# Weights split three groups ahead in five buffers, and the merge's bias tiles on SP's queue, in a hybrid RWKV and attention block

## Chip, cores and metric

The kernel runs on one core of a Trainium2 chip. The metric is the device time of one execution in microseconds (us); of several runs the median is given.

## What is computed

One residual layer on 256 tokens with 2048 channels, in float32. Two token mixers (RWKV-7 and banded chunk attention) share one normalised input and one large input projection; their gated outputs are projected, merged by sigmoid gates and projected once more.

```python
h = _rms_norm(x, pre_norm_g)
proj = h @ w_in                          # 2048 x 12288
p_r, p_k, p_v, z_r, q_a, k_a, v_a, z_a, m_r, m_a = split(proj)
y_r = _rwkv7_mixer(h, p_r, p_k, p_v, ...) * silu(z_r)
y_a = _chunk_band_attention(q_a, k_a, v_a, rel_bias) * silu(z_a)
u_r = y_r @ w_branch_rwkv;  u_a = y_a @ w_branch_attn
merged = sigmoid(m_r + b_merge[0]) * u_r + sigmoid(m_a + b_merge[1]) * u_a
x = x + _rms_norm(merged @ w_out, post_norm_g)
```

## The kernel before

All large products run on TensorE (PE) in float32r, and each float32 operand is split into a high part and a low part so that three products of the parts give the accuracy. The weights come from HBM in groups of 512 KB (four tiles of 128x256, or two of 128x512). One group goes through three hands: SP's queue loads it into a `raw` tile (`w_load`, line 87, `wide_chunks`, line 93; three buffers, NR), ScalarE (ACT) copies it to the high part `wh`, and VectorE (DVE) subtracts to get the low part `wl` (both in `split`, line 80). `wh` and `wl` have NH and NL buffers each. A `raw` tile comes free when both have read it, a pair `wh`, `wl` when PE has used it.

The products are listed in a plan (`product`, line 250) in this order: k0 and r0 (interleaved, on the un-normalised input), v0, lora (the low-rank decay and rate weights), then k, r and v of head pairs 2, 4 and 6, then the gates and the attention's q, k and v in the order of `ORDER`, then the merge (per 512 columns: mr, ma, ur, ua) and the output (o0 to o4). A name such as wh_k03 is the high part of group 3 of product k0; acc_k0 is its accumulator in PSUM. `run_plan` walks over the groups and, before the matmuls of group n, calls `prepare` for all groups up to n + 2. Between groups it pumps small steps of the recurrence and of the attention. The order on each engine in the built program is then set by a scheduler that works with a model of times of its own, so instructions of neighbouring groups can change places; on the chip each engine keeps the built order, and waits where an operand is late.

Names at the start: `hr_A`, `hr_yrl`, `hr_yrh` are the split raw input (16 tiles, from loads of `xT_UV` and `xT_R`), `hn` the normalised one, `lab`, `lab_Y`, `lab_s` the low-rank weights, `rb` and `rones` the norm's factor, `w2e`, `zw` and `lw` the decay's second product. In the middle, `SB` is the recurrent state, `pw` and `pu` products of its chain. In the merge, `bb` is a bias row of b_merge, spread over all partitions by the load (`load_bias`, line 949); it is added to the accumulator on line 967.

Of the kernel before, what the change touches and what calls it, by code (L numbers as in the profile page):

```python
# [9 lines left out]
F32 = mybir.dt.float32  # L10
# [12 lines left out]
BD = 1  # L23

NR = 3
NH = 4
NL = 4

ZI = 6

# [7 lines left out]
P = 128  # L38
D = 2048
# [22 lines left out]
def kernel(ctx: ExitStack, tc, x, xt, vecs, w_in, wa1, w2, a2, w0, rel, w_br, w_ba, w_out, post_g, bm, out):  # L62
    nc = tc.nc
# [5 lines left out]
    tp = ctx.enter_context(tc.tile_pool(name="tp", bufs=2))  # L69
# [4 lines left out]
    def small(name):  # L74
        return ps.tile([P, 512], F32, tag="sm", name=name)
# [4 lines left out]
    def split(h, l, src):  # L80
        ACT.activation(h, src, AF.Copy)  # L81
        DVE.tensor_tensor(l, src, h.bitcast(F32), op=ALU.subtract)  # L82
# [153 lines left out]
    def pump(n):  # L236
        nonlocal turn
        turn += 1
        step(side, n)
        if turn % BD == 0:  # L240
            step(back, BQ)
# [8 lines left out]
    def product(nm, raws, act, token_major, done=None, quota=1, before=None, wide=False, first=False):  # L250

        plan.append(dict(nm=nm, raws=raws, act=act, tm=token_major, done=done, quota=quota, before=before, wide=wide, first=first))
# [4 lines left out]
    def matmuls(acc, q, m, kk, k, wh, wl, first, last):  # L259
        a = q["act"](kk)  # L260
        ms = slice(m * P, (m + 1) * P)
        o = acc[:, m, 0:256]
        pair = not isinstance(a, tuple)
        if q["wide"]:
            wh, wl = (t.rearrange("p k c -> p (k c)").rearrange("p (k c) -> p k c", k=2) for t in (wh, wl))
            o = acc[:, m, :]
        if q["tm"]:
            ah, al = (a[:, 0, :], a[:, 1, :]) if pair else a
            ops = ((o, ah[:, ms], wh[:, k, :]), (o, ah[:, ms], wl[:, k, :]), (o, al[:, ms], wh[:, k, :]))
        elif pair:  # L270
            ops = ((acc[:, m, :], wh[:, k, ms], a.rearrange("p n t -> p (n t)")), (o, wl[:, k, ms], a[:, 0, :]))
        else:
            ops = ((o, wh[:, k, ms], a[0]), (o, wh[:, k, ms], a[1]), (o, wl[:, k, ms], a[0]))
        for n, (d, u, v) in enumerate(ops):
            PE.matmul(d, u, v, start=first and n == 0, stop=last and n == len(ops) - 1)  # L275

    def run_plan():

        steps = [(q, g) for g in range(4) for q in plan[:2]] + [(q, g) for q in plan[2:] for g in range(len(q["raws"]))]
        parts = {}  # L280

        def prepare(n):
            q, g = steps[n]
            if q is plan[-1] and g == len(q["raws"]) - 1:

                wh = bg.tile([P, 4, 256], F32R, tag="v", name="wh_last")
                wl = bg.tile([P, 4, 256], F32R, tag="bon", name="wl_last")
            else:
                wh, wl = (st.tile([P, 4, 256], F32R, tag=t, name=f"{t}_{q['nm']}{g}", bufs=n) for t, n in (("wh", NH), ("wl", NL)))
            raw = q["raws"][g]  # L290
            if hasattr(raw, "whole"):
                raw(wh, wl)
            else:
                split(wh, wl, raw())
            parts[n] = (wh, wl)

        ready = 0
        for n, (q, g) in enumerate(steps):
            while ready < len(steps) and ready <= n + 2:
                prepare(ready)  # L300
                ready += 1
            if g == 0:
                if q["before"]:
                    q["before"]()
                if q["first"]:
                    q["acc"] = small(f"acc_{q['nm']}").rearrange("p (m t) -> p m t", m=2)
                else:
                    q["acc"] = pm.tile([P, 2, 512], F32, tag="mm", name=f"acc_{q['nm']}")
            acc = q["acc"]
            ng = len(q["raws"])  # L310
            if q is plan[-1]:
                if g == ng - 1:
                    for m in range(2):

                        o = acc if not m else small("acc_last").unsqueeze(1).to_broadcast([P, 2, 512])
                        for kk in range(4 * ng):
                            matmuls(o, q, m, kk, kk % 4, *parts[n - ng + 1 + kk // 4], kk == 0, kk == 4 * ng - 1)
                        q["done"](o, m)
            elif q["wide"]:
                for m in range(2):  # L320
                    for k in range(2):
                        kk = 2 * g + k
                        matmuls(acc, q, m, kk, k, *parts[n], kk == 0, kk == 2 * ng - 1)
            else:
                if isinstance(q["act"](0), tuple) or q["tm"]:
                    cuts = [range(k, k + i) for k, i in FIRST] if n == 0 else (range(4),)
                else:

                    cuts = ()
                    wh, wl = parts[n]  # L330
                    for low in range(2):
                        for m in range(2):
                            for k in range(4):
                                a = q["act"](4 * g + k)
                                ms = slice(m * P, (m + 1) * P)
                                if low:
                                    PE.matmul(acc[:, m, 0:256], wl[:, k, ms], a[:, 0, :], start=False, stop=g == ng - 1 and k == 3)  # L337
                                else:
                                    PE.matmul(acc[:, m, :], wh[:, k, ms], a.rearrange("p n t -> p (n t)"), start=g == 0 and k == 0, stop=False)  # L339
                for ks in cuts:  # L340
                    for m in range(2):
                        for k in ks:
                            kk = 4 * g + k

                            one = q["first"]
                            matmuls(acc, q, m, kk, k, *parts[n], kk == 0 and (m == 0 or not one), kk == 4 * ng - 1 and (m == 1 or not one))
            if q is not plan[-1]:
                pump(q["quota"])
                if g == ng - 1 and q["done"]:
                    q["done"](acc)  # L350
# [580 lines left out]
    def start_merge():  # L931
        drain()
        mg.append(bg.tile([P, KT, T], F32R, tag="A", name="mgh"))
        mg.extend(bg.tile([P, KB, T], F32R, tag=t, name=f"mgl_{t}") for t in ("AB0", "yrl"))
# [11 lines left out]
    for c in range(4):  # L946
        ts = {}

        def load_bias(w, c=c, ts=ts):
            def f():  # L950
                if not (c or w):
                    start_merge()
                bb = tp.tile([P, 512], F32, tag="bb", name=f"bb{w}{c}")
                ts["b"] = bb
                nc.scalar.dma_start(bb, bm[w * D + c * 512:w * D + (c + 1) * 512].partition_broadcast(P))
                if not w:
                    if c % 2:
                        ts[0], ts[1] = (bg.tile([P, 2, 512], F32, tag=t, name=f"g{c}_{t}") for t in ("Y", "bon"))
                    else:
                        g = bg.tile([P, 2, 2, 512], F32, tag="yrh", name=f"g{c}")  # L960
                        ts[0], ts[1] = g[:, 0], g[:, 1]
            return f

        def dm(w, c=c, ts=ts):
            def f(acc):
                t = ts[w]
                DVE.tensor_tensor(t, acc, ts["b"].unsqueeze(1).to_broadcast([P, 2, 512]), op=ALU.add)
                ACT.activation(t, t, AF.Tanh, scale=0.5)
            return f

        def du(w, c=c, ts=ts):
            def f(acc):
                DVE.scalar_tensor_tensor(ts[w], ts[w], 1.0, acc, op0=ALU.add, op1=ALU.mult)
                if w:
                    DVE.tensor_tensor(ts[0], ts[0], ts[1], op=ALU.add)
                    back.append(turn_merged(c, ts[0]))
            return f

        def wide(nm, src, k0, act, done, before=None):
            product(nm, wide_chunks(src, k0, nm), act, True, done, before=before, wide=True)  # L980
        wide(f"mr{c}", w_in, O_MR + c * 512, h_norm, dm(0), load_bias(0))
        wide(f"ma{c}", w_in, O_MA + c * 512, h_norm, dm(1), load_bias(1))
        wide(f"ur{c}", w_br, c * 512, yr, du(0))
        wide(f"ua{c}", w_ba, c * 512, lambda k: ya[k // 4][:, k % 4], du(1))
# [93 lines left out]
```

## Time and profile before

| what | us |
|---|---|
| median of 3 runs (862.5, 862.61, 866.8) | 862.61 |
| the profiled execution's own time | 863.52 |
| its span, from first to last instruction | 861.8 |
| PE busy in the span | 842.4 |
| DVE busy | 572.6 |
| ACT busy | 425.4 |

The stages in the span: the start with k0, r0, v0, lora and k2 up to some 75 us, the other products of the mixers up to 490, the merge up to 764, the output product up to 854, and a tail of 8 us in which the last columns are normalised and stored. A busy share near one says that PE has work in flight, not that nothing could be faster. The views used below are the sums of each engine, PE's list of waits, stretches with the granted clock, and the instructions of one engine in order of time. A timeline row gives start, duration, engine, line, operation, operands with shapes, count, and in brackets the idle time ahead of it with what ended it.

### The profile page before, as it was taken

What the parts mean: (1) busy time and instruction counts of PE and PEld (TensorE: products, weight loads), DVE (VectorE), ACT (ScalarE), POOL (GpSimd) and SP (SyncE); (2) the same over time, 40 slices, a digit from 0 to 9 for tenths busy, and PEclk for the clock granted to TensorE, in tenths of its full rate; (3) what the DMA queues carried; (4) which work ended last, traced back from release to release, by engine and by line L of the source; (5) the groups of instructions that cost most, each with busy time, mean ns of one, the idle gap of its engine ahead of it and who ended that gap; (6) DMA issues with size and microseconds to landing.
All of it is one profiled execution on the core that took longest, in us unless ns stands there. A gap on an engine that the chain in (4) does not pass through costs nothing.

```text
span 861.8 us, 14000 instructions
## 1 busy us (share of the span) xinstructions
PE 842.4 (98%) x5624; PEld 714.7 (83%) x5624; DVE 572.6 (66%) x801; ACT 425.4 (49%) x600; POOL 17.2 (2%) x68
## 2 busy tenths in 40 slices
PE   7999999999899999999999999999999999999996
PEld 7998888888778888888888877888888888888896
DVE  7898996966647978645498776555564555565555
ACT  7558565536335554343456655444444444444442
POOL 2010000000000000000000000000000000000000
PEclk9999999999899999999999999999999999999999
DMA  9916634654243556633436545666666666675552
GB/s 296 249 46 194 195 124 137 198 170 133 72 125 99 172 154 208 201 123 123 146 124 197 170 130 172 205 181 204 208 195 198 202 206 225 221 251 197 194 187 99
DMA packets 119395, 149.35 MB, mean 173 GB/s; under 512 B 13601, under 2 KB 82209, under 8 KB 118946
## 3 DMA queue, kind: packets, MB, share of 16 engines
q1 hardware_dynamic: 114370, 139.48, 51.5%
q10 hardware_dynamic: 4960, 8.98, 3.3%
q8 instruction: 44, 0.72, 0.3%
q14 instruction: 21, 0.17, 0.1%
HBM read 145.82 MB, written 2.62 MB: 172 GB/s over the span
## 4 chain that ended last, share of the span: by engine, by line
PE 93%; DVE 2%; DMA 2%; SPq 1%; issue 0%; ACT 0%; DVEq 0%
PE acc_mr L275 10%; PE acc_ma L275 10%; PE acc_o L275 10%; PE acc_va L275 5%; PE acc_ua L275 5%; PE acc_ur L275 5%; PE acc_zr L339 4%; PE acc_q L339 4%; PE acc_za L339 3%; PE acc_ak L339 3%; PE acc_v L339 3%; PE acc_r L339 3%; PE acc_za L337 2%; PE acc_zr L337 2%; PE acc_q L337 2%; PE acc_k L339 2%
## 5 line engine op out<-in xcount | busy, mean ns | idle before, releaser
L275 PE MATMUL acc_mr<-wh_mr,hn 128*128 128x512 f32 x256 | 81.0, 392 | 0.0
L275 PE MATMUL acc_ma<-wh_ma,hn 128*128 128x512 f32 x256 | 79.9, 391 | 0.0
L82 DVE TENSOR_TENSOR wl_ma<-raw_ma,wh_ma 128x1024 fp32r<-128x1024 f32 x32 | 39.2, 1224 | 37.6 <-ACT wh_ma L81 37.6
L82 DVE TENSOR_TENSOR wl_o<-raw_o,wh_o 128x1024 fp32r<-128x1024 f32 x31 | 37.9, 1224 | 35.0 <-ACT wh_o L81 35.0
L82 DVE TENSOR_TENSOR wl_mr<-raw_mr,wh_mr 128x1024 fp32r<-128x1024 f32 x32 | 39.1, 1223 | 31.0 <-ACT wh_mr L81 30.9
L275 PEld LDWEIGHTS acc_mr<-wh_mr,hn 128*128 128x128 f32 x256 | 48.0, 188 | 10.3 <-issue 0.5
L275 PEld LDWEIGHTS acc_ma<-wh_ma,hn 128*128 128x128 f32 x256 | 47.8, 188 | 10.1 <-issue 0.3
L81 ACT ACTIVATE wh_ma<-raw_ma 128x1024 fp32r<-128x1024 f32 x32 | 33.9, 1060 | 42.8 <-PE acc_mr L275 17.5
L81 ACT ACTIVATE wh_mr<-raw_mr 128x1024 fp32r<-128x1024 f32 x32 | 33.9, 1061 | 42.1 <-PE acc_ua L275 18.1
L81 ACT ACTIVATE wh_o<-raw_o 128x1024 fp32r<-128x1024 f32 x31 | 32.9, 1060 | 41.6 <-PE acc_o L275 26.5
L275 PE MATMUL acc_mr<-wl_mr,hn 128*128 128x512 f32 x128 | 50.2, 392 | 0.0
L275 PE MATMUL acc_o<-wh_o,mgh 128*128 128x512 f32 (+1 forms) x140 | 49.9, 356 | 0.0
L275 PE MATMUL acc_ma<-wl_ma,hn 128*128 128x512 f32 x128 | 49.8, 389 | 0.0
L275 PE MATMUL acc_o<-wl_o,mgh 128*128 128x512 f32 (+1 forms) x140 | 49.8, 356 | 0.0
L275 PE MATMUL acc_va<-wh_va,hn 128*128 128x512 f32 x128 | 41.0, 398 | 0.0
L339 PE MATMUL acc_q<-hn,wh_q 128*128 128x512 f32 x128 | 34.0, 401 | 0.0
L339 PE MATMUL acc_zr<-hn,wh_zr 128*128 128x512 f32 x128 | 33.7, 402 | 0.3 <-DVE ak L384 0.3
L339 PE MATMUL acc_ak<-hn,wh_ak 128*128 128x512 f32 x128 | 33.6, 398 | 0.3 <-DVE aq L384 0.3
L339 PE MATMUL acc_za<-hn,wh_za 128*128 128x512 f32 x128 | 33.8, 398 | 0.0
L82 DVE TENSOR_TENSOR wl_ua<-raw_ua,wh_ua 128x1024 fp32r<-128x1024 f32 x16 | 19.6, 1223 | 18.0 <-ACT wh_ua L81 18.0
L82 DVE TENSOR_TENSOR wl_ur<-raw_ur,wh_ur 128x1024 fp32r<-128x1024 f32 x16 | 19.6, 1223 | 17.9 <-ACT wh_ur L81 17.9
L82 DVE TENSOR_TENSOR wl_va<-raw_va,wh_va 128x1024 fp32r<-128x1024 f32 x16 | 19.5, 1222 | 17.2 <-ACT wh_va L81 15.8
(481 smaller groups left out, 2094.5 us busy)
## 6 DMA issues: line engine op xcount, KB each, us to landing
raw_mr<-w_in_d SPq DMA_DIRECT2D x32, 512.0 KB, 4.5
raw_ma<-w_in_d SPq DMA_DIRECT2D x32, 512.0 KB, 3.6
raw_o<-w_out_d SPq DMA_DIRECT2D x32, 512.0 KB, 4.7
raw_v<-w_in_d SPq DMA_DIRECT2D x16, 512.0 KB, 3.7
raw_q<-w_in_d SPq DMA_DIRECT2D x16, 512.0 KB, 3.6
raw_ak<-w_in_d SPq DMA_DIRECT2D x16, 512.0 KB, 3.6
raw_zr<-w_in_d SPq DMA_DIRECT2D x16, 512.0 KB, 3.7
raw_va<-w_in_d SPq DMA_DIRECT2D x16, 512.0 KB, 3.6
```

Source lines behind the costliest of these rows:

```text
L81: ACT.activation(h, src, AF.Copy)
L82: DVE.tensor_tensor(l, src, h.bitcast(F32), op=ALU.subtract)
L275: PE.matmul(d, u, v, start=first and n == 0, stop=last and n == len(ops) - 1)
L337: PE.matmul(acc[:, m, 0:256], wl[:, k, ms], a[:, 0, :], start=False, stop=g == ng - 1 and k == 3)
L339: PE.matmul(acc[:, m, :], wh[:, k, ms], a.rearrange("p n t -> p (n t)"), start=g == 0 and k == 0, stop=False)
```

## The change

Three things change. `wh` and `wl` get five buffers each instead of four, and `prepare` runs up to group n + 3 instead of n + 2. The eight bias tiles of the merge leave their own tag `bb` (two buffers of 2 KB per partition) and take the two buffers of tag `xs`, which the token shift and the gates zr2, zr0 and zr4 used before. And their loads are issued on SP's queue, where the weights are loaded, instead of ACT's.

```diff
-NH = 4
-NL = 4
+NH = 5
+NL = 5
@@ run_plan
-            while ready < len(steps) and ready <= n + 2:
+            while ready < len(steps) and ready <= n + 3:
@@ load_bias
-                bb = tp.tile([P, 512], F32, tag="bb", name=f"bb{w}{c}")
+                bb = tp.tile([P, 512], F32, tag="xs", name=f"bb{w}{c}", bufs=2)
                 ts["b"] = bb
-                nc.scalar.dma_start(bb, bm[w * D + c * 512:w * D + (c + 1) * 512].partition_broadcast(P))
+                nc.sync.dma_start(bb, bm[w * D + c * 512:w * D + (c + 1) * 512].partition_broadcast(P))
```

Before, the loads of the first two bias tiles stand on ACT's queue among its first activations, ahead of wh_k00 and of wh_r00. After, they stand on SP's queue, the first ahead of the load raw_ak43, the second ahead of raw_za62, and the other six in the merge, some six groups ahead of the bias's use. On SP's queue at the start, the load raw_v02 now stands ahead of w2e and not behind it.

PE at the start, where k0 and r0 end and v0 begins, before:

```order
L275 MATMUL acc_r0_235<-hr_yrl_79,wl_r02_299 128x256
L275 MATMUL acc_k0_202<-hr_yrh_80,wh_k03_333 128x256 x2
L275 MATMUL acc_r0_235<-hr_yrh_80,wh_r03_371 128x256 x2
L275 MATMUL acc_k0_202<-hr_yrh_80,wl_k03_334 128x256
L275 MATMUL acc_k0_202<-hr_yrh_80,wh_k03_333 128x256 x2
```

The same place after:

```order
L275 MATMUL acc_r0_249<-hr_yrl_79,wl_r02_275 128x256
L275 MATMUL acc_k0_210<-hr_yrh_80,wh_k03_309 128x256 x2
L275 MATMUL acc_r0_249<-hr_yrh_80,wh_r03_347 128x256 x2
L275 MATMUL acc_v0_509<-hr_A_78,wh_v00_383 128x256 x2
L275 MATMUL acc_k0_210<-hr_yrh_80,wl_k03_310 128x256
L275 MATMUL acc_k0_210<-hr_yrh_80,wh_k03_309 128x256 x2
```

The first two matmuls of v0, which need wh_v00, moved from behind all 24 matmuls of group k03 to a place ahead of its low part. (In the same way the first two of r01 moved ahead of wl_k01, and `rb` moved some 14 matmuls back.)

DVE from the split of lora2 on, where the normalised input is made, before:

```order
L82 TENSOR_TENSOR wl_lora2_626<-lab_Y_379,wh_lora2_625 128x1024
L370 SCALAR_TENSOR_TENSOR xT_R_82<-xT_R_82,vt_75,rones_106 128x256 x2
L82 TENSOR_TENSOR hn_656<-xT_UV_81,hn_656 128x4x256
L370 SCALAR_TENSOR_TENSOR xT_R_82<-xT_R_82,vt_75,rones_106 128x256
L82 TENSOR_TENSOR hn_656<-xT_UV_81,hn_656 128x4x256
L82 TENSOR_TENSOR wl_lora3_664<-lab_s_380,wh_lora3_663 128x1024
L82 TENSOR_TENSOR hn_656<-xT_R_82,hn_656 128x4x256
```

After:

```order
L370 SCALAR_TENSOR_TENSOR xT_R_82<-xT_R_82,vt_75,rones_106 128x256
L82 TENSOR_TENSOR wl_lora3_632<-lab_s_356,wh_lora3_631 128x1024
L740 SCALAR_TENSOR_TENSOR r0_498<-xsr0_495,vt_75,r0_498 128x256 x2
L82 TENSOR_TENSOR hn_662<-xT_UV_81,hn_662 128x4x256
L370 SCALAR_TENSOR_TENSOR xT_R_82<-xT_R_82,vt_75,rones_106 128x256
L82 TENSOR_TENSOR wl_k20_670<-raw_k20_671,wh_k20_669 128x1024
```

The low part of lora3 moved ahead of all four splits of `hn`; it stood behind two of them. The splits of k20 to k23 moved up too, between those of `hn`.

PE where k2 ends, r2 begins and the decay's product `lw` stands, before:

```order
L275 MATMUL acc_k2_785<-hr_yrh_80,wh_k23_818 128x256 x2
L455 MATMUL lw00_810<-w2e_157,zw_158 128x512
L455 MATMUL lw01_814<-w2e_157,zw_158 128x512
L466 MATMUL pn0_862<-pn0h_858,onesr_112 128x512
L275 MATMUL acc_k2_785<-hr_yrh_80,wl_k23_819 128x256
L339 MATMUL acc_r2_968<-hn_656,wh_r20_878 128x512 x8
```

After:

```order
L275 MATMUL acc_k2_791<-hr_yrh_80,wh_k23_785 128x256 x2
L275 MATMUL acc_k2_791<-hr_yrh_80,wl_k23_786 128x256
L339 MATMUL acc_r2_974<-hn_662,wh_r20_824 128x512 x7
L455 MATMUL lw00_816<-w2e_157,zw_158 128x512
L455 MATMUL lw01_820<-w2e_157,zw_158 128x512
L466 MATMUL pn0_868<-pn0h_864,onesr_112 128x512
L339 MATMUL acc_r2_974<-hn_662,wh_r20_824 128x512
```

Seven matmuls of r20 moved ahead of `lw`. What makes `zw`, which `lw` reads, now has one more split ahead of it on each engine: wl_r21 on DVE, and wh_r22 on ACT. From k43 on, PE's order is the same as before up to the last product.

## Rows read from the trace of the kernel before

**Rows 1.** The profile's first part: busy time, share and instructions of each engine.

```profile
PE 842.4 (98%) x5624; PEld 714.7 (83%) x5624; DVE 572.6 (66%) x801; ACT 425.4 (49%) x600; POOL 17.2 (2%) x68
```

**Rows 2.** PE's waits by releaser: us in total, times, longest us.

```profile
PE pw L662 <- DVE SB L695: 1.8, 1, 1.8
PE acc_k L275 <- DVE wl_k L82: 1.6, 3, 0.8
PE acc_k L275 <- ACT wh_k L81: 1.5, 2, 1.2
...
PE lw L455 <- issue: 1.1, 1, 1.1
PE acc_lora L275 <- DVE wl_lora L82: 1.0, 1, 1.0
```

**Rows 3.** Stretches: busy PE, PEld, DVE, ACT, POOL; granted clock, DMA share, GB/s.

```profile
13.00:27.00 14.00, 13.24 (x108) 12.84 (x107) 12.25 (x19) 9.57 (x15) 0.00 (x0) 1.00 1.11 340
27.00:31.00 4.00, 2.68 (x18) 2.06 (x17) 3.49 (x5) 2.19 (x3) 0.00 (x0) 1.00 1.11 237
...
216.30:219.70 3.40, 1.44 (x31) 1.04 (x27) 3.32 (x7) 0.38 (x1) 0.00 (x0) 1.00 0.13 21
219.70:226.50 6.80, 6.16 (x83) 5.60 (x83) 6.15 (x13) 2.86 (x6) 0.00 (x0) 0.51 0.19 69
...
566.00:764.00 198.00, 198.00 (x887) 164.24 (x886) 108.42 (x93) 85.70 (x84) 0.00 (x0) 1.00 0.65 208
...
853.50:861.80 8.30, 0.43 (x4) 0.22 (x2) 3.77 (x7) 1.49 (x4) 1.46 (x1) 0.78 0.56 203
```

**Rows 4.** ACT in order of time, in the first 75 us.

```profile
4.46 0.35 ACTq L955 DMA_DIRECT2D bb<-bm_d  x1
...
6.12 0.41 ACTq L955 DMA_DIRECT2D bb<-bm_d  x1
...
24.64 1.71 ACT L145 ACTIVATE hr_yrh<-xT_R,vt 128x256 fp32r<-128x256 f32 x4 [3.15 <-DMA xT_R<-xt_d]
...
31.73 1.06 ACT L81 ACTIVATE wh_v<-raw_v 128x1024 fp32r<-128x1024 f32 x1 [2.54 <-DMA raw_v<-w_in_d]
...
72.62 0.42 ACT L424 ACTIVATE zw<-lz 64x256 f32<-64x256 f32 x1
```

**Rows 5.** Section 6 of the page: a DMA issue, its count, KB and us to landing.

```profile
bb<-bm_d ACTq DMA_DIRECT2D x8, 256.0 KB, 4.5
```

**Rows 6.** PE in order of time, at the start.

```profile
29.25 0.50 PE L275 MATMUL acc_r<-hr_yrh,wh_r 128*128 128x256 f32 x2 [0.44 <-ACT wh_r L81]
30.35 0.39 PE L275 MATMUL acc_k<-hr_yrh,wl_k 128*128 128x256 f32 x1 [0.60 <-DVE wl_k L82]
...
33.09 0.40 PE L275 MATMUL acc_v<-hr_A,wh_v 128*128 128x256 f32 x2
...
57.75 0.39 PE L275 MATMUL acc_lora<-hr_yrh,wl_lora 128*128 128x256 f32 x1 [1.04 <-DVE wl_lora L82]
...
73.13 1.96 PE L455 MATMUL lw<-w2e,zw 65*128 65x512 f32 x4 [1.10 <-issue]
...
75.28 1.99 PE L339 MATMUL acc_r<-hn,wh_r 128*128 128x512 f32 x8
```

**Rows 7.** DVE in order of time, at the start, near 217 us, and in the merge.

```profile
28.74 0.42 DVE L411 TENSOR_TENSOR lab_Y<-lab_Y,vt 128x256 f32<-128x256 f32 x1 [0.18 <-DMA lab_Y<-wa_d]
29.08 1.22 DVE L82 TENSOR_TENSOR wl_k<-raw,wh_k 128x1024 fp32r<-128x1024 f32 x1
...
56.49 1.21 DVE L82 TENSOR_TENSOR wl_lora<-lab_s,wh_lora 128x1024 fp32r<-128x1024 f32 x1
...
216.98 1.22 DVE L82 TENSOR_TENSOR wl_zr<-raw_zr,wh_zr 128x1024 fp32r<-128x1024 f32 x1
...
588.90 1.22 DVE L967 TENSOR_TENSOR g_Y<-acc_mr,bb 128x1024 f32<-128x1024 f32 x1 [0.40 <-PE acc_mr L275]
```

**Rows 8.** The chain that ended last, in the merge: start, duration, what.

```profile
588.86 21.76 PE acc_ma L275 x96
```

## The prediction, made before the changed kernel was run

> **What bounds the kernel.** I read the sums of the engines first. PE is busy for 842.4 of 861.8 us [rows 1], so all idle time of PE together is 19.4 us, and nothing in this change takes a matmul away. Then where these 19.4 us lie. After 853.5 us PE is busy for 0.43 of 8.30 [rows 3]: some 7.9 us are the tail after the last matmul, which the change does not touch. The rest, 11.5 us, is PE's list of waits; its largest entries [rows 2] lie at the start (weights of k0 and r0, lora's last group, `lw`) and at one place in the middle, where the recurrence waits for its state SB. The merge has no idle time at all: PE is busy for 198.00 of 198.00 us from 566 to 764 [rows 3]. A weight that is ready a group sooner is worth something only where PE waits for weights, and that is the start.
>
> One more loss stands in the stretches. From 219.7 to 226.5 us the granted clock is 0.51, which is the level of 1.2 GHz, and it is 1.00 (2.4 GHz) in every other stretch of rows 3 but the tail. Ahead of the fall PE had been busy for only 1.44 of 3.40 us, waiting for SB [rows 2, 3]. At half speed, 6.80 us give about 0.49 x 6.80 = 3.3 us less work. So the middle costs some 5 us, the wait and the clock together.
>
> **The sum's base.** The profiled execution took 863.52 us for a span of 861.8. The terms below are differences in the span, and I put them on the median of the runs, 862.61.
>
> **Steady state: nothing.** With five buffers and a lead of three groups, the split of group n+1 stands where that of group n stood, and waits for the same matmuls to free its buffers. DVE and ACT do the same work at the same times, on a group one later. That holds in the middle too. Before SB's update DVE still has a split to do, at the place of the one at 216.98 [rows 7]; it is now va00's and not zr23's, of the same size. So I leave the wait for SB and the fall of the clock as they are. What hides the third group of lead is that two were enough, outside of the start.
>
> **Term 1, the weights of k0, r0 and v0.** Two things act against each other. (a) The bias loads at 4.46 and 6.12 [rows 4] leave the start: 2 x 256 KB [rows 5], at the 340 GB/s that the DMA engines move from 13 to 27 us, with their share full [rows 3], are 1.5 us. What lands after some 13 us should land up to that much sooner, for instance the last input tiles, for which ACT waited 3.15 us until 24.64 [rows 4]. (b) PE's order is worse: the first two matmuls of v0 stand ahead of the low part of k03. Before, that low part began at 30.35, when DVE had made it, and v0 came at 33.09 [rows 6]. Now PE cannot pass v0 until wh_v00 is there; that activation began at 31.73 on the landing of raw_v00, and took 1.06 [rows 4], so 32.8 before. I bound it. Latest: no gain from (a), 32.8. Earliest: lab_Y lands at 28.7 [rows 7], raw_v00 follows 512 KB or 1.5 us later at the full rate (the rate fell to 237 GB/s there [rows 3], with w2e's load in the stream, which now comes one load later), less 1.5 from (a), plus 0.1 and 1.06 for ACT: 29.9. I take 30.4, nearer to the early end, because the stream was full until 27 us and the bias bytes were in it. Before, from 30.35 PE needed 33.09 - 30.35 = 2.74 us for the low stretch of k03 and 0.24 for v0's pair, done at 33.33. After, the pair comes first: 30.4 + 0.24 + 2.74 = 33.4. So term 1 is 0.0 us, with ends of -0.5 and +2.4. The gain from the bias loads is eaten by the order.
>
> By the Trainium skill (DMA: Bandwidth & Descriptors, "Issuing engines are not separate DMA queues"), loads issued by different engines run on the same 16 DMA engines and interleave. By that rule the change of queue would bring nothing by itself, and (a) would come wholly from the later time of the two loads; the full share in rows 3 agrees, and the sum stays.
>
> **Term 2, lora.** At 57.75 PE had waited 1.04 us for the low part of lora3 [rows 6]; DVE made it at 56.49, behind two splits of `hn` of 1.21 us each [rows 7]. It now stands ahead of both, 2.4 us sooner, which more than covers the wait: -1.04. What is late next are the splits of k20 to k23, which moved up as well.
>
> **Term 3, lw.** At 73.13 PE had waited 1.10 us [rows 6] for `zw`, made on ACT at 72.62 in 0.42 [rows 4]. Now seven matmuls of r20, of 1.99 / 8 = 0.25 us or a little less each [rows 6], some 1.6 us, stand ahead of it on PE as cover. Against it, `zw` has the split wl_r21 (1.2 us) and wh_r22 (1.06) more ahead of it. But these are fed by loads that can start only when k22 and k23 are split, and these splits come sooner. I take the cover as sufficient: -1.1. If both splits come at their old pace, `zw` is 2.3 us later, at 75.3; PE, with the 1.04 of term 2 and the 1.6 us of r20 done, stands in front of it, and of terms 2 and 3 together +0.6 is left (75.3 against 73.13 + 1.6 = 74.7). So the two together are -2.1, ends -2.1 and +0.6.
>
> **Term 4, the merge's loads.** Six loads of 256 KB, 0.75 us each at 340 GB/s, go through SP's queue among the weights, where PE has a lead of three groups of 21.76 / 8 = 2.72 us [rows 8]. I take 0, covered by that lead; without it, see the third rival.
>
> **Sum.** 0.0 - 1.0 - 1.1 = -2.1, so 862.6 - 2.1 = 860.5 us; by the bounds 862.6 - 2.6 = 860.0 to 862.6 + 3.0 = 865.6.
>
> **Rivals.** (1) The clock falls at the start; the slower side. Ahead of v0's pair PE would do only two pairs of matmuls (0.5 us) between about 27.9 and 30.4, so it is idle for some 2.0 of 2.5 us, and for longer if raw_v00 is late. Before, 1.32 of 4.00 us idle (27 to 31) left the clock at 1.00, and 1.96 of 3.40 idle (216.3 to 219.7) came ahead of its fall [rows 3]. [...] Price 3.3 us: 863.8, and with v0 at its latest, 866.2, slower than before. For it: the size of the idle stretch. Against it: the stretch is short if raw_v00 lands at the early end. (2) The fall in the middle is missed: PE comes to the wait for SB a few us sooner, and the clock stays up. -3.3: 857.2. [...] The Trainium skill (TensorE: Matmul & The Clock Gate, "What's actually happening") says that the gate's watch runs freely and does not start with the kernel; by that, the same idle stretch can bring a fall in one run and not in another, which no row here shows. (3) The bias loads hold up the weights. SP takes its queue in order, and a bias load waits for the DVE addition that frees its buffer (1.22 us, after the last matmul of a product [rows 7]); the next group's load is behind it. Where the lead of 8.2 us is used up, each of the six costs 1.2 + 0.75 = 2 us: 860.5 + 12 = 872.5. Against it: the next load has to wait for a split that ends about as late as that addition. By the Trainium skill (DMA: Bandwidth & Descriptors, "Anatomy of one DMA") a wait sits on the issuing sequencer and not in the DMA engines, which is the mechanism of this rival. (4) The lead does nothing: what PE gains until 75 us it waits for further on, since DVE paces the start. No change, 862.6.
>
> **How the numbers follow.** Forecast 0.42, rival 1 0.32, rival 2 0.14, rival 3 0.04, rival 4 0.08. The likeliest is 860.5. A range from 856.9 to 864.8 takes in rivals 1, 2 and 4 at their centres and leaves out rival 3 and the late end of rival 1. A measurement of this kernel can tell about 0.5%, or 4.3 us, from no change: faster is below 858.3, slower above 866.9. Faster has rival 2 and a rest of the forecast's low end, 0.18; slower has rival 3 and the late end of rival 1, 0.07; the same, 0.75.
>
> **What would show it.** Right: PE waits in front of v0's first pair near 28 to 30.4 us, with wh_v as the releaser; no wait at lora3; a wait under 0.5 us at `lw`; the same wait for SB and the same stretch at half clock near 215 to 225; 198 of 198 us busy in the merge. Wrong: a stretch at 0.5 of the clock after 30 us (rival 1), none near 220 (rival 2), PE idle in the merge behind a weight (rival 3), or waits for `wl` between 75 and 125 us (rival 4).

## The result and the profile after

The changed kernel took 859.0 us in the median of five runs (858.32 to 860.16), the kernel before 863.35 beside it: a ratio of 0.9946, with a 95% interval of 0.9928 to 0.9964. In a later group of runs (e5 below) it was 859.92 against 864.44, 0.9954 (0.9936 to 0.9972). So the kernel is about 0.5% faster, 4.4 us. The prediction had 860.5, a gain of 2.1 us on a base of 862.61 from three runs; the five runs beside the changed kernel put that base at 863.35. The time lies in the predicted range, the gain is twice as large. The profiled execution took 858.43 us for a span of 856.7, against 863.52 and 861.8 before.

The sums of the engines on the page of the changed kernel (busy time, share, instructions):

```profile
PE 839.7 (98%) x5624; PEld 712.5 (83%) x5624; DVE 571.3 (67%) x801; ACT 424.7 (50%) x600; POOL 18.2 (2%) x68
```

Busy PE fell by 2.7 us against [rows 1] with the same instructions, the idle time by 2.4 us (19.4 to 17.0). The stretches of the changed kernel, with the columns of [rows 3], and one more stretch at the start:

```profile
9.00:12.00 3.00, 2.23 (x17) 1.82 (x16) 2.16 (x3) 3.00 (x6) 0.00 (x0) 1.00 1.09 349
13.00:27.00 14.00, 13.93 (x114) 13.52 (x113) 13.61 (x22) 11.71 (x17) 0.00 (x0) 1.00 1.11 337
27.00:31.00 4.00, 2.83 (x24) 2.63 (x24) 4.00 (x5) 1.83 (x2) 0.00 (x0) 1.00 0.90 202
...
216.30:219.70 3.40, 2.12 (x52) 1.86 (x52) 3.09 (x7) 1.46 (x4) 0.00 (x0) 1.00 0.32 122
219.70:226.50 6.80, 6.61 (x71) 5.46 (x69) 4.17 (x8) 2.65 (x5) 0.00 (x0) 1.00 0.01 2
566.00:764.00 198.00, 198.00 (x888) 164.18 (x887) 105.86 (x92) 84.85 (x84) 0.00 (x0) 1.00 0.65 211
```

Three things differ from [rows 3]. DVE is busy for 13.61 of 14.00 us from 13 to 27 (12.25 before) and for all 4.00 from 27 to 31 (3.49 before): its data come sooner. PE is busy for 13.93 (13.24 before). And in this execution the granted clock is 1.00 from 216 to 226 us, where it was 0.51 from 219.7 on before. The merge is full in both.

PE's longest waits in the changed kernel (us in total, times, longest):

```profile
PE pw L662 <- DVE SB L695: 1.8, 1, 1.8
PE acc_k L275 <- ACT wh_k L81: 1.2, 1, 1.2
PE acc_v L275 <- ACT wh_v L81: 1.2, 1, 1.2
```

Against [rows 2], `lora` and `lw` have left the list, and the wait for wh_v in front of v0's first pair is new. Further down the list the wait for UV behind SB has grown from 0.2 to 1.0 us. ACT and then PE at the start, in order of time:

```profile
20.95 1.71 ACT L145 ACTIVATE hr_yrh<-xT_R,vt 128x256 fp32r<-128x256 f32 x4 [1.02 <-DMA xT_R<-xt_d]
...
27.86 1.06 ACT L81 ACTIVATE wh_v<-raw_v 128x1024 fp32r<-128x1024 f32 x1 [1.34 <-DVE wl_k L82]
...
70.61 0.42 ACT L424 ACTIVATE zw<-lz 64x256 f32<-64x256 f32 x1
```

```profile
28.97 0.51 PE L275 MATMUL acc_v<-hr_A,wh_v 128*128 128x256 f32 x2 [1.17 <-ACT wh_v L81]
29.32 0.28 PE L275 MATMUL acc_k<-hr_yrh,wl_k 128*128 128x256 f32 x1
...
31.95 0.28 PE L275 MATMUL acc_r<-hr_yrh,wl_r 128*128 128x256 f32 x1
...
55.17 0.28 PE L275 MATMUL acc_lora<-hr_yrh,wl_lora 128*128 128x256 f32 x1
...
69.33 1.77 PE L339 MATMUL acc_r<-hn,wh_r 128*128 128x512 f32 x7
71.13 1.96 PE L455 MATMUL lw<-w2e,zw 65*128 65x512 f32 x4
```

Read with [rows 4] and [rows 6]: the last input tiles are there 3.7 us sooner (20.95 against 24.64), wh_v begins at 27.86 and not at 31.73, PE reaches the low part of k03 1.0 us sooner (29.32 against 30.35) in spite of its 1.17 us in front of v0, passes lora3 2.6 us sooner and without a wait (55.17 against 57.75), and does seven matmuls of r20 ahead of `lw`, which then needs no wait. The fair place to compare the start is the low part of r03, since by then v0's pair and k03 are done in both orders. It begins at 31.95 after and at 33.33 before, 1.38 us sooner:

```profile
33.33 0.28 PE L275 MATMUL acc_r<-hr_yrh,wl_r 128*128 128x256 f32 x1
```

### The profile page after: what moved, and what is told of

Read it like the earlier page. It is cut to its first block, busy times and chain, and to the rows that moved or that the text cites. A ratio compares the mean times of both kernels' runs of the same rounds, so it can differ in the third digit from the quotient of the medians.

```text
span 856.7 us, 14014 instructions
## 1 busy us (share of the span) xinstructions
PE 839.7 (98%) x5624; PEld 712.5 (83%) x5624; DVE 571.3 (67%) x801; ACT 424.7 (50%) x600; POOL 18.2 (2%) x68
## 4 chain that ended last, share of the span: by engine, by line
PE 94%; DVE 2%; SPq 2%; DMA 1%; ACT 1%; issue 0%; DVEq 0%
PE acc_mr L275 10%; PE acc_ma L275 10%; PE acc_o L275 10%; PE acc_va L275 5%; PE acc_ua L275 5%; PE acc_ur L275 5%; PE acc_q L339 4%; PE acc_zr L339 4%; PE acc_za L339 3%; PE acc_ak L339 3%; PE acc_v L339 3%; PE acc_r L339 3%; PE acc_za L337 2%; PE acc_zr L337 2%; PE acc_q L337 2%; PE acc_ak L337 2%
## 5 line engine op out<-in xcount | busy, mean ns | idle before, releaser
L81 ACT ACTIVATE wh_ak<-raw_ak 128x1024 fp32r<-128x1024 f32 x16 | 16.9, 1058 | 29.1 <-PE acc_q L339 13.4
```

## The experiments

In each group of runs the kernel before ran on the same chip; its medians were 863.70 (e1 to e4), 864.44 (e5 to e8), 864.69 (e9 to e11) and 863.38 (e12). Ratios are to it. The changed kernel itself ran again only beside e6 to e8 (as e5), so e1 to e4 and e9 to e12 are set against it by way of these ratios. The edits are shown abridged.

| run | what | us | ratio, 95% interval |
|---|---|---|---|
| e1 | before, bias tiles moved only | 862.27 | 0.9981 (0.9967 to 0.9994) |
| e2 | changed, two early loads put back | 864.46 | 1.0011 (0.9994 to 1.0027) |
| e3 | changed, lead of two groups | 860.97 | 0.9961 (0.9946 to 0.9976) |
| e4 | changed, v0 behind k03 | 861.41 | 0.9981 (0.9967 to 0.9994) |
| e5 | changed, once more | 859.92 | 0.9954 (0.9936 to 0.9972) |
| e6 | changed, one split on POOL | 861.40 | 0.9971 (0.9961 to 0.9982) |
| e7 | before, one split on POOL | 864.49 | 1.0010 (0.9992 to 1.0028) |
| e8 | changed, bias on ACT's queue | 859.95 | 0.9950 (0.9930 to 0.9970) |
| e9 | changed, split behind UV | 857.99 | 0.9928 (0.9902 to 0.9953) |
| e10 | before, split behind UV | 863.44 | 0.9984 (0.9963 to 1.0006) |
| e11 | changed, lw ahead of r20 | 861.20 | 0.9970 (0.9949 to 0.9991) |
| e12 | e9 and r * k behind UV | 859.90 | 0.9950 (0.9932 to 0.9969) |

### e1 and e2: the bias loads alone, and the fifth buffers alone

e1 is the change without its first half (NH and NL are 4, the lead is two). e2 is the changed kernel with the two early loads back:

```diff
+    early = bg.tile([P, 2, 512], F32, tag="AB0", name="early")
@@ first_raw
+                if g == 0:
+                    nc.scalar.dma_start(early[:, k // 2, :], bm[k * 256:k * 256 + 512].partition_broadcast(P))
                 split(wh[:, k:k + n, :], wl[:, k:k + n, :], raw[:, k:k + n, :])
```

> Four buffers and the old lead, as in the kernel before; only the bias tiles are moved (tag xs, SP's queue, out of the start). Theory (three separate gains at the start): only the loads' part is there. PE reaches the low part of k03 about 1.0 us sooner than before and stays 1.4 us sooner through v0; the wait for wl_lora3 (1.0 us) and for lw (1.1 us) are still there. Some 1.4 us less than before, 861.9 where before has 863.35. Rival (one gain: the early loads hold up everything that follows, and the rest is a consequence): lora and lw come 2.6 to 3.5 us sooner as in the changed kernel, 859.9.

> The changed kernel with two more loads of 256 KB each, issued on ACT's queue among its first activations, where the kernel before issued its first two bias loads, into a tile that nothing reads. Theory (three separate gains): the gain of the sooner landings goes, wl_k03 is back at about 30.4 us, while wl_lora3 still stands ahead of the splits of hn and has no wait (-1.0); lw stands without the matmuls of r20 ahead of it here, so its wait of some 1.1 us is back. 1 us less than before, 862.3. Rival (the order with five buffers carries the whole gain): as the changed kernel within 1 us, 859 to 860.

The time of e1 came out as the theory had it, 1.4 us less than before. The first row on ACT, and then PE at lora3 and in front of `lw`:

```profile
20.42 1.71 ACT L145 ACTIVATE hr_yrh<-xT_R,vt 128x256 fp32r<-128x256 f32 x4 [0.88 <-DMA xT_R<-xt_d]
```

```profile
54.52 0.39 PE L275 MATMUL acc_lora<-hr_yrh,wl_lora 128*128 128x256 f32 x1
...
70.31 2.35 PE L455 MATMUL lw<-w2e,zw 65*128 65x512 f32 x4 [1.49 <-issue]
```

The input lands as in the changed kernel, and the wait for `lw` has stayed (1.10 us before, [rows 6]). But the profile does not bear the theory out at lora3: the wait that was to stay there is gone, although DVE still makes wl_lora3 behind two splits of `hn`. PE passes lora3 3.2 us sooner than before (54.52 against 57.75) and comes to `lw` 2.8 us sooner, as the rival had it. In this execution most of that was lost again: the granted clock was 0.80 from 72 to 80 us with PE busy throughout, some 1.6 us of its work, and PE waited 0.66 us near 180 us for a block that comes back from HBM. So the gains at the start are not three separate ones. The new order of v0's pair ahead of k03 is there in e1 as well, so it comes from the loads' move and not from the buffers. e2 missed: 1.0 us less than before was expected, 0.8 more was measured, with an interval of -0.5 to +2.3 us, which does not tell it from the kernel before. Its rows:

```profile
22.27 1.71 ACT L145 ACTIVATE hr_yrh<-xT_R,vt 128x256 fp32r<-128x256 f32 x4 [1.70 <-DMA xT_R<-xt_d]
```

```profile
58.62 0.48 PE L275 MATMUL acc_k<-hr_A,wh_k 128*128 128x256 f32 x2 [1.17 <-DVE xsv L381]
...
71.01 1.95 PE L455 MATMUL lw<-w2e,zw 65*128 65x512 f32 x4 [1.61 <-issue]
```

There is no wait at lora3, but PE waits 1.17 us in front of k2, whose accumulator comes free when DVE has read v0's (`xsv`), and 1.61 us in front of `lw`. So the two halves do not add up: each alone takes away the wait at lora3, each alone keeps the wait for `lw`, and only together PE's order puts r20 ahead of it. In the profiles the first matmul of `pw` that waits for SB stands at 218.58 us before, 217.99 in e1, 217.40 in e2, and 214.93 with both, in one execution each; in e5, the changed kernel once more, it stands at 213.92. That e2 is 1.2 us ahead at this place and yet no faster in its median stays open.

### e3 and e8: the written lead, and the queue

e3 changes `n + 3` back to `n + 2` and keeps five buffers; e8 writes `nc.scalar` for `nc.sync` in `load_bias` and keeps the rest.

> The changed kernel with five buffers, but prepare up to n + 2 as before. In the built program PE, ACT and POOL have the same order as in the changed kernel; DVE has one split of v0 at another place, SP one load of v0. Theory (the fifth buffer sets what can be ahead, the written lead does not): as the changed kernel, 859.0 within 0.7 us. Rival (the lead of three groups brings it): 2 us of the gain are gone, 861.

> The changed kernel with its bias loads issued on ACT's queue instead of SP's; tiles and buffers as in the changed kernel, and the order of PE, DVE and POOL the same. Theory (what counts is when the two first bias tiles are loaded, not by which queue): as the changed kernel within 0.7 us, PE busy without a gap in the merge. Rival (on ACT the bias loads are ready early again and land in the start, or they delay the high parts on ACT): the gain of the start goes, 861 to 863.

e3 (0.9961) and e8 (0.9950) lie within the intervals of the changed kernel. e3's 860.97 us is 2 us above the expected 859.0 and where its rival had it, but the kernel before took 863.70 in that group; by the ratios e3 is 0.6 to 1.3 us slower than the changed kernel, which is within the noise. The written lead and the queue bring nothing that these runs can tell: the built order depends on which buffer is free, and e3's order on PE is the changed kernel's; what counted of the loads was their time, not who issued them.

### e4: the order of v0's pair

```diff
@@ run_plan, ahead of the first matmul of v0
+    with tc.issue_after(last matmul of k03), tc.issue_after(last matmul of r03):
```

> The changed kernel, but PE's first two matmuls of v0 stand behind all of k03 and r03, as in the kernel before, and not ahead of the low part of k03. Theory (the order costs what PE waits in front of v0): the wait of 1.17 us for wh_v00 near 29 us goes, PE starts the low part of k03 at about 28.1 us instead of 29.3, and keeps 1.0 us: 858.0. Rival (DVE paces what follows, PE waits the same time further on, in front of v0 or lora): 859.0, no difference, with a new wait of about 1 us between 30 and 60 us.

The theory failed. The wait in front of v0 went, and PE started k03's low part straight behind the first pair of r03, though at 28.83 and not at 28.1 (the granted clock was 0.58 from 12 to 16 us in this execution). But k2 began no sooner:

```profile
28.83 0.28 PE L275 MATMUL acc_k<-hr_yrh,wl_k 128*128 128x256 f32 x1
```

```profile
57.80 0.47 PE L275 MATMUL acc_k<-hr_A,wh_k 128*128 128x256 f32 x2
```

In the changed kernel k2 begins at 57.81, and the instruction on DVE that frees its accumulator is `xsv`, which ends at 57.5:

```profile
56.81 0.68 DVE L381 TENSOR_TENSOR xsv<-acc_v,rones 128x512 f32<-128x512 f32 x1
```

In e3 and e2, where PE came there sooner, it waited for `xsv` for 0.80 and 1.17 us. So in this order of DVE `xsv` sets the earliest start of k2, and what PE saves beyond that is lost there. I take the gain of the early loads to be that DVE, not PE, has its data sooner; no run changes that alone. e4's median is 1.5 and 2.4 us above the two of the changed kernel; its interval (0.9967 to 0.9994) overlaps one of theirs and not the other. The edit also moved a split of lora2 and one of `hn` on DVE, and in the profiled execution PE waited 1.5 us for the block that comes back from HBM (last section), for which it did not wait in the changed kernel. Whether the edit itself makes e4 slower stays open.

### e5 to e7: does the clock fall, and what does the wait for SB cost?

e5 is the changed kernel again. In e6 and e7 one split goes to POOL (`va0`, group 0 in the changed kernel; `zr2`, group 3 in the kernel before):

```diff
-        DVE.tensor_tensor(l, src, h.bitcast(F32), op=ALU.subtract)
+        eng.tensor_tensor(l, src, h.bitcast(F32), op=ALU.subtract)   # POOL for this one group
```

> The changed kernel once more, beside the other runs of this group. Its first five runs gave 859.0 in the median and fell into two sorts: 858.3 and 858.4 with a mean granted clock of 0.998, and 859.0 to 860.2 with 0.993 to 0.997. Theory (the clock falls in some executions and not in others): the median lies between 859 and 861, the runs at 0.998 at 858.4, and a run with one fall of 7 us costs some 1.4 us more. Rival (the fall is a fixed part of a kernel's run): the profile has again no stretch at half clock between 200 and 230 us, and all runs lie within 0.5 us of 859.0.

> The changed kernel, but the one split that stands ahead of SB's update on DVE near 213 us (wl_va00, 1.22 us) is made by POOL, which is idle there; all other instructions keep their order. Theory: SB's update starts 1.1 to 1.2 us sooner, PE's wait in front of pw falls from 1.8 to about 0.7 us, and the clock stays at 1.00 there in every run: 1.2 us less than the changed kernel where its clock held, about 2 us less in the median, 857.5. Rival (the wait moves on to the next link, UV or W, or POOL is late with the split): the wait for UV grows by the same 1.1 us, no difference from the changed kernel.

> The kernel before, but its split ahead of SB's update (wl_zr23, 1.22 us near 217 us) is made by POOL. Theory: the wait for SB falls from 1.8 to about 0.7 us and the stretch at half clock after it goes; 1.2 for the wait and 1.4 for the clock, 861.1 where the kernel before has 863.7. If one fall had the price that the prediction gave it (3.3 us), 859.2. Rival (the clock falls all the same): 862.5.

e5 settles the first question. Its wait for SB is the same 1.82 us, and this time the clock fell, as the stretch (columns as in [rows 3]) shows:

```profile
215.30:218.70 3.40, 2.54 (x45) 2.29 (x47) 3.09 (x7) 1.46 (x4) 0.00 (x0) 0.64 0.35 132
```

So the same wait in the same kernel brings a fall in one execution and none in another. The Trainium skill (TensorE: Matmul & The Clock Gate, "What's actually happening") says that the watch behind the gate runs freely and does not reset with the kernel; these two executions agree with it. The price of a fall is read from the first matmul behind SB to the first of the next large product, in the changed kernel, in e5 and in the kernel before:

```profile
214.93 1.14 PE L662 MATMUL pw<-SB,AB 128*64 128x64 f32 x16 [1.82 <-DVE SB L695]
...
221.06 2.11 PE L339 MATMUL acc_zr<-hn,wh_zr 128*128 128x512 f32 x8
```

```profile
213.92 1.14 PE L662 MATMUL pw<-SB,AB 128*64 128x64 f32 x16 [1.82 <-DVE SB L695]
...
220.34 2.12 PE L339 MATMUL acc_zr<-hn,wh_zr 128*128 128x512 f32 x8
```

```profile
218.58 1.14 PE L662 MATMUL pw<-SB,AB 128*64 128x64 f32 x16 [1.82 <-DVE SB L695]
...
225.54 2.64 PE L339 MATMUL acc_zr<-hn,wh_zr 128*128 128x512 f32 x8
```

That is 6.13 us at full clock, 6.42 in e5, and 6.96 in the kernel before, whose eight matmuls of zr then take 0.53 us more: 0.3 to 1.4 us for a fall. Other profiles bear this out: in e1, e3, e4 and e8, where the clock fell there too, the same way took 6.97 or 6.98 us, and in e2, where it did not, 6.12. The rest of the chain there is DVE's and ACT's time: behind SB, PE waits 1.04 us for UV at full clock and 0.17 in the kernel before at half clock, so what PE loses it mostly waits less. The runs fit, though a mean clock counts falls at every place and a longer wait lengthens a run by itself. Of 97 runs of the kernel before in these groups, the 8 with a mean granted clock of 0.997 or 0.998 took 862.7 us in the mean, the 32 with 0.993 or 0.994 863.9, the 35 with 0.991 or 0.992 864.6, the 13 at 0.990 or lower 866.6. From the first to the second of these groups, 4 thousandths of the clock would be 3.4 us of PE's time and go with 1.2 us; the lowest group lies further off.

e6 and e7 failed. The wait for SB grew to 2.7 us. e6, DVE, POOL and PE in order of time, and behind them DVE's same instruction in the changed kernel:

```profile
210.62 3.44 DVE L530 SCALAR_TENSOR_TENSOR AB<-kk,iv 64x512 f32<-64x512 f32 x2
```

```profile
211.02 2.50 POOL L82 TENSOR_TENSOR wl_va<-raw_va,wh_va 128x1024 fp32r<-128x1024 f32 x1 [51.20 <-ACT wh_va L81]
```

```profile
215.07 1.57 PE L662 MATMUL pw<-SB,AB 128*64 128x64 f32 x16 [2.74 <-DVE SB L695]
```

```profile
211.40 1.39 DVE L530 SCALAR_TENSOR_TENSOR AB<-kk,iv 64x512 f32<-64x512 f32 x2
```

While POOL worked, DVE's pair of instructions took 3.44 us instead of 1.39, 2.05 more than usual, so the 1.22 us that the move saved on DVE were more than lost. In e7 it is the same pair, 3.45 us. The move did not take the cause away.

### e9 and e10: the wait for SB, without POOL

```diff
@@ group_back
-            DVE.tensor_copy(UV[HS[0], 0, :, c], puv[HS[0]])
+            marks[f'UV{g}{c}'] = DVE.tensor_copy(UV[HS[0], 0, :, c], puv[HS[0]]).ins
@@ split, for va0's group 0 (e9) or zr2's group 3 (e10)
+        with tc.issue_after(marks['UV01']):
             DVE.tensor_tensor(l, src, h.bitcast(F32), op=ALU.subtract)
```

> The changed kernel, but on DVE the split wl_va00 stands behind the copy of UV that follows SB's update, and not ahead of SB; every other instruction of every engine keeps its place. No POOL work is added, so DVE has no partner to wait for. Theory: SB's update starts 1.1 us sooner, the wait in front of pw falls from 1.8 to about 0.7 us, the next waits (W 0.5, UV 0.6 to 1.0) stay as they are: 1.1 us less than the changed kernel, and the clock falls there in fewer of the runs. 858.6 where the changed kernel has 859.9. Rival (the chain ends at the same time, since UV's copy stands behind the same DVE work): the wait for UV grows by 1.1 us, no difference.

> The kernel before with the same single move: the split wl_zr23 behind the copy of UV instead of ahead of SB's update. Theory: the wait for SB falls from 1.8 to about 0.7 us, 1.1 us less than the kernel before, and where the clock holds afterwards some 1.4 us more: 863.0 to 861.8 where the kernel before has 864.2. If a fall of the clock had the price of the prediction (3.3 us) and stayed away, 859.8. Rival: no difference, the wait goes to UV.

In both the wait fell as the theory had it. One instruction of DVE is at another place; e9 on DVE, then on PE, and PE in e10:

```profile
212.50 0.87 DVE L695 TENSOR_TENSOR SB<-pg,f 64x256 f32<-64x256 f32 x2
...
216.43 0.41 DVE L670 COPY UV<-pu 64x256 f32<-64x256 f32 x1
216.78 1.21 DVE L82 TENSOR_TENSOR wl_va<-raw_va,wh_va 128x1024 fp32r<-128x1024 f32 x1
```

```profile
212.96 1.14 PE L662 MATMUL pw<-SB,AB 128*64 128x64 f32 x16 [0.69 <-DVE SB L695]
...
216.90 0.33 PE L682 MATMUL pg<-UV,BT 128*64 128x64 f32 x2 [1.03 <-DVE UV L670]
```

```profile
219.30 1.14 PE L662 MATMUL pw<-SB,AB 128*64 128x64 f32 x16 [0.69 <-DVE SB L695]
```

The wait for SB is 0.69 us in both, and in e9 the wait for UV has not grown (1.04 us in the changed kernel). e9 has the lowest median: 857.99 us, 0.9928 of the kernel before; against the changed kernel (0.9946 and 0.9954) that is some 1.6 to 2.2 us by the ratios, but the intervals overlap and the two did not run side by side. What the profiles show is the wait itself, 1.1 us less (1.82 and 0.69). In neither profile did the clock fall there. e10 gains 1.25 us in the median; its interval reaches just past 1, so by the times alone this gain is not shown. A fall at the prediction's price of 3.3 us would have made it 859.8; it was 863.4.

### e11: the cover of lw

```diff
@@ run_plan, r2, group 0
+    with tc.issue_after(marks['lw01']):
         PE.matmul(acc[:, m, :], wh[:, k, ms], ...)
```

> The changed kernel, but the two matmuls lw stand ahead of all matmuls of r20 again, as in the kernel before; the rest of the start as in the changed kernel. Theory (term 3 of the prediction, the seven matmuls of r20 are the cover of zw): PE waits 1.5 to 1.8 us in front of lw near 69 us, and the time is that much longer, 861.5 where the changed kernel has 859.9. Rival (what follows is paced by DVE and ACT, the wait is made up by 115 us): within 0.5 us of the changed kernel.

By the medians the time is 1.3 us longer than in e5, 0.9970 against 0.9954 by the ratios, in the direction of the theory; the intervals overlap, so the times do not show it. In its profile the wait in front of `lw` was 0.70 us, less than expected, since ACT made `zw` 1.5 us sooner in that execution than in the changed kernel's first profile (PE, then ACT):

```profile
69.61 1.96 PE L455 MATMUL lw<-w2e,zw 65*128 65x512 f32 x4 [0.70 <-issue]
```

```profile
69.10 0.42 ACT L424 ACTIVATE zw<-lz 64x256 f32<-64x256 f32 x1
```

### e12: one link more

```diff
@@ duo_front, j0 = 4
+        with tc.issue_after(marks['UV01']):
             DVE.scalar_tensor_tensor(r[:, m, :], ...)
```

> The kernel of the run before (split wl_va00 behind the copy of UV), and in addition DVE's product r * k (two instructions, 0.88 us, near 215.5 us) behind that copy too. The order of PE changes in the products behind it (zr2 and va0, where pw of the third chunk is moved). Theory (the recurrence's chain is paced by what DVE has ahead of each link): the wait for UV falls from 1.0 to about 0.2 us, 0.8 us less than the run before, 857.2 where that had 858.0. Rival (the gain is lost to the other order of zr2 and va0, or to the clock): 858 to 859, with a new wait between 220 and 250 us.

The rival was right that the gain is lost. The wait for UV is gone, but the new order puts SB's next update ahead of the read of q's accumulator, and PE's list of waits has it in its second place:

```profile
PE acc_zr L339 <- DVE aq L384: 1.1, 1, 1.1
```

In this profile the clock fell there as well (0.66 from 216 to 220 us), although the wait for SB was 0.68 us as in e9. The time was 859.90 us, 0.9950: no better than the changed kernel, and e9 keeps the lowest median.

## Why the prediction was right, and where it was not

**Bound and steady state.** Right as far as shown. PE is full in the merge, e3 does not show that the third group of lead is worth anything by itself, and the gain lies in the start; the wait in the middle stayed as it was, 1.82 us.

**Term 1 (0.0 us, ends -0.5 and +2.4).** This is the step that failed: it was put at nothing, and it measured -1.38 us at the low part of r03 (33.33 to 31.95). The loads alone (e1) gave -1.4 us in time, but with the wait at lora3 gone as well. Two sizes in the term were wrong. (a) The gain of the landings was put at 1.5 us, the bytes by the full rate; the last input tiles came 3.7 us sooner (20.95 against 24.64), and 4.2 in e1, while the two loads of e2, of the same size and on the same queue, cost 1.3 against the changed kernel (22.27 against 20.95). This is not an accident of one execution: the tiles came at 24.08 and 24.67 in e10 and e7, which have the early loads, and between 20.31 and 21.14 in the eight other kernels without them. Most of it was there when SP issued the load of these tiles, 2.4 us sooner (before, then after):

```profile
15.65 1.42 SPq L139 DMA_DIRECT2D xT_R<-xt_d  x1
```

```profile
13.27 1.42 SPq L139 DMA_DIRECT2D xT_R<-xt_d  x1
```

Why the two loads on ACT's queue hold up SP's issues by that much is open. A part shows in the rate: from 9 to 12 us the DMA engines moved 349 GB/s in the changed kernel and 293 in the kernel before,

```profile
9.00:12.00 3.00, 1.67 (x11) 1.47 (x12) 2.21 (x3) 3.00 (x6) 0.00 (x0) 1.00 0.99 293
```

which is 0.17 MB or 0.5 us beyond the bytes. The other 1.7 us stay open. (b) So wh_v00 was assumed at 30.4, between the bounds of 29.9 and 32.8; it was done at 28.92 (27.86 + 1.06), sooner than both. PE waited in front of v0 for 1.17 us, as the mechanism said, but until 28.97 and not until 30.4. In e4, without this order, k2 began no sooner (57.80 against 57.81), so the order cost nothing there.

**Term 2 (-1.04).** Right in its place and size: no wait at lora3, and PE's lead over the kernel before, 1.4 us at r03, is 2.6 us there, 1.2 more. The reason given for it, DVE's new order, is not needed: in e1 the wait went with the old order, by the sooner loads alone. And e2 shows that the gain is kept only where DVE's `xsv` comes sooner as well; else PE waits the same time in front of k2.

**Term 3 (-1.1).** Right: no wait at `lw`, with the seven matmuls of r20 as its cover. `zw` came at 70.61, behind one more split, as the bound feared; these splits had moved up. The cover was just enough: `zw` was done at 71.03 and PE began `lw` at 71.13. Without the cover (e11) PE waited 0.70 us; the 1.3 us between the medians is not clear of the noise.

**Term 4 (0).** Right, PE is busy for 198.00 of 198.00 us in the merge, on either queue (e8).

**The sum.** -2.1 was predicted. Ahead of any fall of the clock the gain is 3.65 us at the wait for SB (218.58 to 214.93): about 1.4 from term 1, 1.2 from term 2 and 1.1 from term 3. The runs agree: at a mean clock of 0.997 or 0.998 the changed kernel took 859.0 in the mean of 7 runs (of its first five and e5) and the kernel before 862.7 in the mean of 8. So nearly all of the 1.5 us by which the sum fell short of this is term 1. The other 0.7 us of the 4.4 between the medians would be the clock's, which no run separates. That the time came within 1.5 us of the predicted 860.5 is in part luck: the base was 0.7 us lower than in the runs beside the changed kernel.

**Rivals.** (1) The clock at the start did not fall behind v0 (1.00 from 27 to 31, PE busy for 2.83 of 4.00). Nor did it in any other profile, though in five of them (e2, e3, e4, e5, e9) it fell between 8 and 16 us. (2) The fall in the middle was missed in the profiled execution, which is the sign that the prediction set for this rival; but in e5 the same kernel had it again, so the change does not rule it out. Whether the change makes falls rarer is open: a mean clock of 0.997 or more had 7 of 17 runs of the changed kernel and 8 of 97 of the kernel before, but the mean also counts falls elsewhere (e5's profile has a second one, 0.60 from 9 to 12 us). The price at this place was 1.4 us at most and not 3.3, since the prediction counted the whole stretch at half clock as lost work, though much of it was waiting for DVE and ACT. The wait itself stayed as it was, as the paragraph on the steady state had it. (3) and (4) did not come: no idle time in the merge, and the gain of the start is still there at 215 us.

## What to carry to other kernels

In this start, where DVE frees the next accumulator, a matmul order that waited 1 us cost nothing that the runs show, and loads that left the start were worth more than their bytes: look which engine frees the next accumulator before costing PE's waits. Price a stretch at half clock by the work that PE is short of in it, not by its length, and do not explain one profile by a fall that may or may not come. A wait that an unrelated instruction causes on DVE was cured here by moving that one instruction behind the chain on the same engine (1.1 us of wait); giving it to POOL made the chain slower.

## What the hardware showed that was not expected

DVE stood still beside POOL: two instructions with two inputs each took 3.44 us instead of 1.39 beside a POOL subtraction of 2.50 us. The first, begun ahead of POOL's, took its usual 0.68 us; the second lost all of the time. The Trainium skill (SBUF — State Buffer, "Who interferes with whom") says that a DVE instruction with two inputs in SBUF contends with a POOL instruction that reads SBUF, and that the later one is blocked, not slowed; the trace agrees, and I had left it out when I expected e6 to help.

A round trip through HBM differs between executions. The recurrence stores a block (line 595) and loads it back when the store is done (line 599); SP's issues of the two, in the changed kernel and in e3:

```profile
339.36 0.34 SPq L595 DMA_DIRECT2D rb<-S  x1
...
342.47 3.78 SPq L599 DMA_DIRECT2D RA<-rb  x8
```

```profile
342.35 0.34 SPq L595 DMA_DIRECT2D rb<-S  x1
...
346.43 3.77 SPq L599 DMA_DIRECT2D RA<-rb  x8
```

3.11 us in one and 4.08 in the other, with the same instructions ahead of them on every engine but for two. In e3 PE then waited 0.75 us for the transposed block, in the changed kernel it did not; in e4's profile such waits make 1.5 us. How much of the 2 to 8 us by which runs of one kernel differ here comes from this and from falls of the clock, no run shows.
